# A two-block float32 model on one core: the filter steps regrouped into the projections, and the recurrence of the first block filled with 16 fixed blocks of other matmuls

## The chip, the core and the metric

The kernel is one program on one core of a Trainium2 chip. The metric is the device time of a run in microseconds (us); three runs of the kernel before have a median of 2095.82 us (2094.42 to 2096.31). A run that was profiled gives a trace: for every engine what ran when, and what it waited for. The engines are PE (TensorE matmuls; PEld is its weight load), DVE (VectorE), ACT (ScalarE), POOL (GpSimd) and SP (SyncE), which in this kernel issues nearly all transfers from HBM. Each engine takes its instructions in the order in which the program has them and waits on semaphores.

## The reference, cut to what matters

256 tokens of width 1024, with 16 meta tokens ahead of them, pass two blocks in float32.

```python
# first block
a = rms_norm(h, norm_mix);  p = a @ w_in                       # 1024 x 4096
y_hy = rms_norm(hyena_mixer(p[:, :1536], ...))                 # short conv, 2 long convs through a spectrum of a learned filter
q, f_fwd, f_bwd, i_in, g = split(p[:, 1536:], 5)               # 5 x 512
f = lb + (1 - lb) * sigmoid(f_fwd or f_bwd); k, log_f = 1 - f, log(f)
o = scan(silu(q), k_f, i_in, lf_f) + flip(scan(flipped ..., k_b, lf_b))   # chunks of 64, 4 heads
y_hg = rms_norm_per_head(o) * norm_w * silu(g)
h = h + concat(y_hy, y_hg) @ w_out
h = h + moe(rms_norm(h, norm_ffn))                             # 64 experts, top 2 of the best of 8 groups
h = rms_norm(h, norm_final)[16:]
# second block: five branches, gates, up and out projection
```

Each expert has three matrices of 1024 x 512, 2 MiB each: 384 MiB are read for the experts.

## The kernel before, in words

A framework places instructions on the engines: it takes the program in its order, plays it through and gives each engine a fixed sequence; a helper `_after` adds an order between two instructions that share no data. Nothing of the order is decided on the chip.

**Mixer** (`_phase_a`). Matmuls that need accuracy are done as three fp32r products of high and low halves (`_mm3`); `_split_w` makes the halves of a weight slice, the high one on ACT (L183), the low one on DVE (L184). In the source's order: `hyena_proj(0)`; the filter, for two orders `o`: taps (`fl` from `hids` and `wsh`, `wsl`, times the window `wn`, split again into `sdh`, `sdl`) and five rows of its spectrum (`fl` from `fs`); `hyena_proj(1)`; `to_freq`; `hyena_proj(2)`; `from_freq`; `forget_proj(0)`; then q, v, and after the pools of this stage are closed `forget_proj(1)`, the recurrence `core(d, t)` four times, `g_proj`, and `out_proj(0)`, `out_proj(1)`, the two halves of `w_out`. In `core`, sums of logarithms (`ep`) go to ACT (exp), DVE (products qd, kd, qb, kl), PE (transposes `tp`), then scores `sp`, state updates `up` and outputs `op`. `tok_proj` makes P of 128 x 512 (`mm`), `out_proj` the same (`mo`).

**Weight buffers.** `_load_w` takes the next buffer of a rota, `k.rings`, and issues its 2 MiB on SP. In the mixer the rota is three buffers of the pool `ring`; `early()`, called when the mixer's first pools are closed, puts the two buffers of `ring2` ahead of them. `_moe` then sets the rota anew and asks for the first tiles in this order:

```python
k.rings[at:at] = [p] * n                                  # early: ring2, ring2, ring, ring, ring
k.rings, k.r3 = [r, k.r2, k.r2, r3, r3, r, r], r3         # _body, ahead of _moe
order = [(x, i) for x in range(3) for i in range(4)]      # gate 0-3, up 0-3, down 0-3 of group 0
first.append(load_g(x, 0, i, {3: spare[0], 4: spare[1], 9: spare[2], 10: spare[3]}.get(n)))
if n: _after(k, k.load, prev)                             # issued on SP in this order
```

So the tiles gate 1 and gate 2 take the two buffers of `ring2`; gate 0, up 3 and down 0 take buffers of `ring`; the spares and `ring3` lie where mixer pools lay. A transfer into a buffer waits until the last split of the weight that lay in it.

**Experts.** 16 groups of four experts: gather of tokens (`xp`), gate and up (`gu`), down (`dn`), scatter (`sc`). In the last group dummy matmuls (`warm`, WD = 14 a time) stand between the four steps of down. `finish` adds the four scattered pieces to `h`, multiplies by a gain (`fan`; t = 0 on DVE, t = 1 on POOL), sums squares on ACT, scales (`an`), transposes and starts the second block's first projection. The **second block** follows.

Of the kernel before, what the change touches and what calls it, by code (L numbers as in the profile page):

```python
# [38 lines left out]
def _consts():  # L39
# [27 lines left out]
    win = np.exp((-tt[:, None] * deltas[None, :]).astype(np.float64)).astype(f)[perm]  # L67
# [134 lines left out]
def _phase_a(k, A, early):  # L202
# [194 lines left out]
    for o in range(2):  # L397
        if o:

            later = w3_sums(o)  # L400
            w3_pair()
        sd = [[sp.tile([128, 2, W], F32R, name=f"sd{n}{i}") for n in "hl"] + [sks[i]] for i in range(2)]
        tm = []
        for kt in (2, 0, 1):
            n = 128 if kt < 2 else NM
            for i, (sh, sl, sk) in enumerate(sd):
                ks = slice(kt * 128, kt * 128 + n)
                p = px([128, W], "fl")
                _mm(k, p[:n], hids[:, ks], wsh[:, i], True, False)
                _mm(k, p[:n], hids[:, ks], wsl[:, i], False, True)  # L410
                t = sp.tile([128, W], F32, name="sdt", bufs=2)
                V.tensor_tensor(t[:n], p[:n], wn[:n, kt], op=OP.mult)
                if kt < 2:
                    nc.scalar.copy(sh[:, kt], t)
                    V.tensor_tensor(sl[:, kt], t, sh[:, kt].bitcast(F32), op=OP.subtract)
                else:
                    tm.append(t)
            if kt == 2:

                V.tensor_tensor(tm[0][0:1], tm[0][0:1], tm[1][0:1], op=OP.add)  # L420
                V.tensor_scalar(tm[0][0:1], tm[0][0:1], 0.5, None, op0=OP.mult)
# [4 lines left out]
        for r in range(5):  # L426
# [8 lines left out]
            nc.scalar.copy(H[o][:m, r], p[:m])  # L435

# [106 lines left out]
    hyena_proj(1)  # L543
# [13 lines left out]
    def bound(n):  # L557

        l = VC[n].rearrange("p (r c) -> p r c", r=2)
        e, m = hp.tile([128, 2, 4], F32, name="lbe"), hp.tile([128, 4], F32, name="lbm")  # L560
# [13 lines left out]
        lb = hp.tile([128, 2, W], F32, name="lb")  # L574
        for r, sg in enumerate((0.5, -0.5)):
            nc.scalar.activation(lb[:, r], p, AF.Copy, scale=sg, bias=0.5)
        return lb

    def forget(p, n, lb, ko, fo):
        e = hp.tile([n, W], F32, name="fe")  # L580
        nc.scalar.activation(e, p, AF.Tanh, scale=0.5)
        V.tensor_tensor(e, e, lb[:n, 1], op=OP.mult)
        V.tensor_tensor(fo, lb[:n, 0], e, op=OP.add)
        V.tensor_tensor(ko, lb[:n, 1], e, op=OP.subtract)

    def forget_proj(d):
        lb = bound(("lb_fwd", "lb_bwd")[d])
        P = tok_proj(hcols(1 + d), d == 0)
        for t in range(2):
            forget(P[t], 128, lb, kk[d][:, t], lf[d][:, t])  # L590
        if d == 0:
            meta_sum(mk, P[2])
            forget(mk, NM, lb, mk, ml)
            x = nc.scalar.activation(ml, ml, AF.Ln)
        y = nc.scalar.activation(lf[d], lf[d], AF.Ln)
        if d == 0:
            _after(k, y, x)

    Y = to_freq(uT[0], H[0])
    hyena_proj(2)  # L600
# [23 lines left out]
    P = tok_proj(hcols(0), False)  # L624
    for t in range(2):
        e = _sigmoid(k, hp, P[t], W, tag="fe")
        V.tensor_tensor(q[:, t], P[t], e, op=OP.mult)
# [9 lines left out]
    P = tok_proj(hcols(3), True)  # L637
    for t in range(2):
        nc.scalar.copy(v[:, t], P[t])
    meta_sum(mv, P[2])  # L640
# [19 lines left out]
    def ustate(lhs, rows, src, srows):  # L660
        p = px([128, 4, 128], "up")
        for h in range(4):
            _mm(k, p[:, h], lhs[rows, HS(h)], src[srows, HS(h)], h == 0, h == 3)
# [4 lines left out]
    def core(d, t):  # L668
# [6 lines left out]
        for nm, mi, sc, src in (("qd", 1, 1.0, q), ("kd", 1, -1.0, kk[d]), ("kl", 2, 1.0, kk[d]), ("qb", 0, 1.0, q)):  # L675
            if nm != "kd":
                p = px([128, W], "ep")
                for i, x in enumerate((hi, lo)):
                    _mm(k, p, B3[d][mi], x, i == 0, i == 1)
            ex = hg.tile([128, W], F32, name="ex", bufs=2)  # L680
            nc.scalar.activation(ex, p, AF.Exp, scale=sc)
            r = hg.tile([128, W], F32, name=nm, tag="kl" if nm == "kl" else "kq", bufs=2)
            kq[nm] = r
            if nm == "kl":
                kl = (r, src[:, t], ex)
                continue
# [12 lines left out]
        p = px([128, 4, 128], "sp")
# [10 lines left out]
        for lc in ((0, 1) if d == 0 else (1, 0)):  # L710
# [5 lines left out]
            p = ustate(kq["kl"], rows, v[:, t], rows)  # L716
            S[d][nx] = hg.tile([128, 4, 128], F32, name="S", bufs=SB)
# [51 lines left out]
    def mix_out(P, half, t, cs):  # L769
# [45 lines left out]
    forget_proj(1)  # L815
# [3 lines left out]
    ex = hg.tile([128, W], F32, name="ex", bufs=2)  # L819
    nc.scalar.activation(ex[:NM], p[:NM], AF.Exp)  # L820
    V.tensor_tensor(mk, mk, ex[:NM], op=OP.mult)
    p = ustate(mk, slice(0, NM), mv, slice(0, NM))
    S[0][0] = hg.tile([128, 4, 128], F32, name="S", bufs=SB)
    V.tensor_copy(S[0][0], p)

    core(0, 0)
    core(1, 1)
    core(0, 1)
    core(1, 0)
    g_proj()  # L830
    w += [_load_w(k, wo[h], 4) for h in range(2)]
    out_proj(0, hyT)
# [45 lines left out]
def _moe(k, A, ctx, ps):  # L878
# [233 lines left out]
    def finish(gT, y):  # L1112
# [25 lines left out]
        def scatter(t, n):  # L1138
            p = ps.tile([128, W], F32, name="sc", tag="px")
            m = q(_mm(k, p, gT[:, t], y[n], True, True))  # L1140
            hs = k.h[:, t, n * W:(n + 1) * W]
            q(V.tensor_tensor(hs, p, hs, op=OP.add))
            return m

        def gained(eng, t, n):
            cs = slice(n * W, (n + 1) * W)
            q(eng.tensor_tensor(fan[:, t, cs], k.h[:, t, cs], k.gains[:, 1, cs], op=OP.mult))

        def squares(t, n):
            for j, src in enumerate((k.h, fan)):  # L1150
                sq = mo.tile([128, W], F32, name="nsq")
                q(ACT.activation(sq, src[:, t, n * W:(n + 1) * W], AF.Square, scale=D ** -0.5, accum_out=f(t, 2 * j + n)))
# [35 lines left out]
        gained(V, 0, 0)  # L1188
        scatter(0, 1)
        gained(V, 0, 1)  # L1190
# [4 lines left out]
        gained(G, 1, 0)  # L1195
# [8 lines left out]
        gained(G, 1, 1)  # L1204
# [12 lines left out]
        for t in range(2):  # L1217
            q(G.tensor_tensor(f(t, 4), f(t, 5), k.mhalf, op=OP.pow))
            q(ACT.activation(k.h[:, t], fan[:, t], AF.Copy, scale=f(t, 4)))

    JS = [slice(j * SLOTS, (j + 1) * SLOTS) for j in range(EP)]
    extra = {4: (0, 0), 6: (0, 1), 8: (1, 0), 10: (1, 1)}
    for g in range(k.ngroups):
# [58 lines left out]
        wm = None  # L1282
        for f in range(4):
# [5 lines left out]
            if g == k.ngroups - 1 and f < 3:  # L1289
                wm = warm_up(WD, m, "px")  # L1290
# [3 lines left out]
        if g == k.ngroups - 1:  # L1294
            finish(gT, y)
# [865 lines left out]
```

## Time and profile before

| what | value |
|---|---|
| runs | 2095.82 us median (2094.42 to 2096.31) |
| the profiled execution | 2094.49 us, its span 2092.7 us |
| granted PE clock, mean of the span | 0.945 |
| mixer | 0 to about 252 us |
| experts | to about 1200 us |
| second block | to the end |

The profile's page gives busy times of the engines over the whole span; windows give them for a stretch, with the granted clock of PE (1.00 is 2.4 GHz, 0.50 is 1.2 GHz), the busy share of the 16 DMA engines and what they moved; a timeline lists instructions in order of time, with the idle time ahead of one in brackets and what ended it.

### The profile page before, as it was taken

What the parts mean: (1) busy time and instruction counts of PE and PEld (TensorE: products, weight loads), DVE (VectorE), ACT (ScalarE), POOL (GpSimd) and SP (SyncE); (2) the same over time, 40 slices, a digit from 0 to 9 for tenths busy, and PEclk for the clock granted to TensorE, in tenths of its full rate; (3) what the DMA queues carried; (4) which work ended last, traced back from release to release, by engine and by line L of the source; (5) the groups of instructions that cost most, each with busy time, mean ns of one, the idle gap of its engine ahead of it and who ended that gap; (6) DMA issues with size and microseconds to landing.
All of it is one profiled execution on the core that took longest, in us unless ns stands there. A gap on an engine that the chain in (4) does not pass through costs nothing.

```text
span 2092.7 us, 24267 instructions
## 1 busy us (share of the span) xinstructions
PE 1847.5 (88%) x10132; PEld 1212.4 (58%) x10132; DVE 919.5 (44%) x1521; ACT 652.1 (31%) x976; POOL 69.6 (3%) x89
## 2 busy tenths in 40 slices
PE   8999987678787787876777799999999999999998
PEld 7877832224232331322222379898788788888886
DVE  6886621021111100111111176756666957756756
ACT  5556400002000100000000154546544645446444
POOL 2000000000000000000000020000000100000000
PEclk9999998789899998988988899999999999999999
DMA  8244899999999999999999954455454355454541
GB/s 278 95 159 146 305 398 428 424 404 415 428 423 428 424 427 428 423 427 423 428 426 428 392 182 161 161 180 182 167 185 166 133 190 179 165 180 171 178 159 55
DMA packets 123265, 593.92 MB, mean 284 GB/s; under 512 B 5951, under 2 KB 7264, under 8 KB 101008
## 3 DMA queue, kind: packets, MB, share of 16 engines
q1 hardware_dynamic: 119008, 583.66, 70.3%
q10 hardware_dynamic: 3376, 5.45, 0.8%
q0 software_dynamic: 768, 3.21, 0.4%
q8 instruction: 82, 1.34, 0.3%
q14 instruction: 31, 0.25, 0.0%
HBM read 591.26 MB, written 1.05 MB: 283 GB/s over the span
## 4 chain that ended last, share of the span: by engine, by line
PE 55%; DMA 21%; DVE 3%; issue 1%; ACT 1%; POOL 0%; ACTq 0%; SPq 0%; DVEq 0%; POOLq 0%
PE pt L141 23%; PE gu L141 10%; DMA wring<-in_w_up 8%; DMA wring<-in_w_down 7%; DMA wring<-in_w_gate 6%; PE pT L141 5%; PE pu L141 5%; PE dn L141 5%; PE pw L141 1%; PE ca L141 1%; DVE wp L184 1%; PE ov L141 1%; PE mk L141 1%; PE xp L141 1%; PE warm L141 0%
## 5 line engine op out<-in xcount | busy, mean ns | idle before, releaser
L141 PE MATMUL pt<-wp,ahl 128*128 128x512 f32 x2160 | 516.8, 397 | 1.7 <-DVE wp L184 1.7
L184 DVE TENSOR_TENSOR wp<-wring,wp 128x1024 fp32r<-128x1024 f32 (+1 forms) x368 | 405.7, 1112 | 238.5 <-ACT wp L183 231.2
L183 ACT ACTIVATE wp<-wring 128x1024 fp32r<-128x1024 f32 (+1 forms) x368 | 353.1, 966 | 350.5 <-PE pt L141 176.5
L141 PEld LDWEIGHTS pt<-wp,ahl 128*128 128x128 f32 x2160 | 403.2, 188 | 93.6 <-DVE wp L184 2.5
L141 PE MATMUL gu<-wring,xg 128*32 128x512 f32 x2016 | 322.4, 680 | 122.9 <-DMA wring<-in_w_up 101.3
L141 PEld LDWEIGHTS gu<-wring,xg 128*32 128x32 f32 x2016 | 75.0, 122 | 341.9 <-issue 163.7
L141 PE MATMUL dn<-wring,hT 128*32 128x512 f32 x992 | 186.0, 686 | 65.7 <-DMA wring<-in_w_down 49.9
L141 PEld LDWEIGHTS dn<-wring,hT 128*32 128x32 f32 x992 | 44.2, 118 | 194.2 <-issue 98.3
L1275 DVE SCALAR_TENSOR_TENSOR hh<-th,gu 128x512 f32<-128x512 f32 x16 | 16.9, 1055 | 308.5 <-PE gu L141 308.5
L1293 DVE COPY ye<-dn 128x512 f32<-128x512 f32 x16 | 11.1, 692 | 276.8 <-PE dn L141 276.8
L141 PEld LDWEIGHTS pT<-ahl,wp 128*128 128x128 f32 x960 | 115.6, 189 | 0.5
L141 PE MATMUL pT<-ahl,wp 128*128 128x256 f32 x960 | 115.8, 283 | 0.0
L1280 ACT COPY hT<-hp 128x512 f32<-128x512 f32 x16 | 9.4, 586 | 295.0 <-PE hp L1278 295.0
L141 PE MATMUL pu<-wp,yTh 128*128 128x512 f32 x320 | 98.9, 397 | 0.8 <-ACT yTh L1459 0.6
L1271 ACT ACTIVATE th<-gu 128x512 f32<-128x512 f32 x16 | 9.5, 596 | 250.5 <-PE gu L141 250.5
L1293 ACT COPY ye<-dn 128x512 f32<-128x512 f32 x16 | 9.4, 586 | 242.0 <-PE dn L141 242.0
L141 PEld LDWEIGHTS xp<-oh,hn 128*128 128x128 f32 x512 | 64.0, 200 | 31.1 <-issue 25.7
L141 PE MATMUL xp<-oh,hn 128*128 128x128 f32 x512 | 68.3, 288 | 7.8 <-PEq L1064 4.6
L141 PEld LDWEIGHTS pu<-wp,yTh 128*128 128x128 f32 x320 | 58.7, 188 | 15.6 <-ACT yTh L1459 3.5
L1272 DVE SCALAR_TENSOR_TENSOR th<-th,gu 128x512 f32<-128x512 f32 x16 | 11.0, 687 | 126.1 <-ACT th L1271 126.1
L141 PE MATMUL pu<-wp,yTl 128*128 128x512 f32 x160 | 61.0, 395 | 0.2
L141 PE MATMUL sc<-ye,gT 128*128 128x512 f32 x128 | 59.3, 606 | 0.0
(539 smaller groups left out, 1995.8 us busy)
## 6 DMA issues: line engine op xcount, KB each, us to landing
wring<-in_w_up SPq DMA_DIRECT2D x73, 2048.0 KB, 18.5
wring<-in_w_in SPq DMA_DIRECT2D x63, 2048.0 KB, 7.8
wring<-in_w_gate SPq DMA_DIRECT2D x63, 2048.0 KB, 19.4
wring<-in_w_down SPq DMA_DIRECT2D x62, 2048.0 KB, 20.9
wring<-in_w_out SPq DMA_DIRECT2D x6, 2048.0 KB, 7.9
wring<-in_w_mem_kv SPq DMA_DIRECT2D x4, 2048.0 KB, 17.0
spare<-in_w_down SPq DMA_DIRECT2D x2, 2048.0 KB, 9.6
wring<-in_w_in SPq DMA_DIRECT2D x4, 512.0 KB, 6.2
```

The costliest lines, as they stand in the source:

```text
L141: return k.nc.tensor.matmul(out, a, b, start=start, stop=stop, skip_group_check=True, **kw)
L183: ih = k.nc.scalar.activation(hi, w[:, a:b], AF.Copy)
L184: il = (eng or k.nc.vector).tensor_tensor(lo, w[:, a:b], hi.bitcast(F32), op=OP.subtract)
L1271: nc.scalar.activation(th, P[0], AF.Tanh, scale=0.5)
L1272: V.scalar_tensor_tensor(th, th, 1.0, P[0], op0=OP.add, op1=OP.mult)
L1275: V.scalar_tensor_tensor(hh, by_f(th), 0.5, by_f(P[1]), op0=OP.mult, op1=OP.mult)
L1280: nc.scalar.copy(hT, p)
L1293: (V.tensor_copy if n else nc.scalar.copy)(y[n], P[n])
```

## The change

Seven edits. (1) Each filter's eight steps (three taps, five rows) are called from inside `hyena_proj(1)` and `hyena_proj(2)`, one a weight slice; the window's factor 0.5 is put into the constant, and `wn` is loaded behind the second projection's weight, in two pieces. (2) The projection of q stands at the first `to_freq`, both bounds ahead of it, both `forget_proj` and v behind it. (3) `forget` is written with one scalar_tensor_tensor and two tensor_scalar, and the three logarithms stand together. (4) g's weight is loaded ahead of `early()`. (5) g's projection and `out_proj(0)` become a generator `fillings` of 8 + 8 blocks of six matmuls, of which `core` takes fixed numbers. (6) `w_out` is loaded from within the generator. (7) In `finish` the rows of `h` are put into PSUM ahead of time by matmuls with the identity, and the scatter adds onto them.

```diff
-    nc.sync.dma_start(wn, A["c_win"])
     wz.append(_load_w(k, win_ap[:, :, W:2 * W]))
+    nc.sync.dma_start(wn[:, :2], A["c_win"][:, :2])
+    nc.sync.dma_start(wn[:NM, 2], A["c_win"][:NM, 2])
...
+    hyena_proj(1, filter_steps(0))
+    later = w3_sums(1)
+    w3_pair()
+    hyena_proj(2, filter_steps(1))
...
+    x = forget_proj(1)
+    for a in (ml, lf[0], lf[1]):
+        x = _after(k, nc.scalar.activation(a, a, AF.Ln), x)
+    P = tok_proj(hcols(3), True)
...
+    wg = hcols(4)
+    ws = [_split_w(k, wg, s, s + 1) for s in range(3)]
...
     early()
...
+        p, m = total(1)
+        expo("qd", p, 1.0, q)
+        expo("kd", p, -1.0, kk[d])
+        m = fill(n["qd"], m)
+        if meanwhile:
+            meanwhile(m)
+        turn("qd", m)
+        turn("kd", m)
+        p, m = total(0)
+        expo("qb", p, 1.0, q)
+        p, m = total(2)
+        expo("kl", p, 1.0, kk[d])
+        turn("qb", fill(n["qb"], m))
...
+        m = fill(n["up"], m)
         for h in range(4):
-            _mm(k, O[t][:, h], scm[d][:, h], v[:, t, HS(h)], h == 0 and not begun[t], False)
+            _after(k, _mm(k, O[t][:, h], scm[d][:, h], v[:, t, HS(h)], h == 0 and not begun[t], False), m)
...
+    def fillings():
+        for c in range(8):
+            x = [triples(P[t], (ah[:, c, o:o + 128], al[:, c, o:o + 128]), (wh[:, 0], wl[:, 0]), c) for t, o in enumerate((NM, NM + 128))]
+            yield x[0][0], x[1][2]
...
+        w.extend(_load_w(k, wo[h], 4) for h in range(2))
+        for n in range(2):
+            parts = [_split_w(k, wn, s, s + 1) for s in range(4)]
+            for t in range(2):
+                for cc in (0, 2):
+                    x = [triples(P[t], (hyT[0][:, c, HS(t)], hyT[1][:, c, HS(t)]), (parts[c][0][:, 0], parts[c][1][:, 0]), c)
+                         for c in (cc, cc + 1)]
+                    yield x[0][0], x[1][2]
...
-    g_proj()
-    w += [_load_w(k, wo[h], 4) for h in range(2)]
-    out_proj(0, hyT)
+    core(0, 0, {"qd": 2, "qb": 1, "up": 1}, meta_state)
+    for c in ((1, 1), (0, 1), (1, 0)):
+        core(*c, {"qd": 1, "qb": 1, "up": 1})
+    for _ in filling:
+        pass
...
+            return q(_mm(k, rows[t, n], gT[:, t], y[n], False, True))
...
+            q(V.tensor_tensor(fan[:, t, cs], rows[t, n], k.gains[:, 1, cs], op=OP.mult))
...
+            p = rows[t, n] = ps.tile([128, W], F32, name="sc", tag="px")
+            behind = _after(k, _mm(k, p, k.ident, k.h[:, t, n * W:(n + 1) * W], True, False), behind)
```

SP's queue, before, from behind the two halves of `w_out` (wring_2135, wring_2137), which are issued just ahead of these rows, into `ring`. wring_1581 is the weight of `forget_proj(1)` and wring_2049 that of g, both in `ring2`; the `in_w_gate`, `in_w_up`, `in_w_down` rows are the first tiles of the experts' group 0.

```order
L2117 DMA wr_1542<-in_w_router 128x576 [waits DMASW2_49,DMASW3_49,PE_49,Activation_49]
L173 DMA wring_1581<-in_w_in 128x8x512
L173 DMA wring_2049<-in_w_in 128x8x512 [waits DMAHW6_49]
L173 DMA wring_2460<-in_w_gate 128x4x1024 [waits DMAHW7_49,DMAHW1_49,DVE_49]
L173 DMA wring_2462<-in_w_gate 128x4x1024 [waits DMAHW5_49,DVE_49]
L173 DMA wring_2464<-in_w_gate 128x4x1024 [waits DMAHW6_49,DVE_49,Activation_49]
L173 DMA spare_2456<-in_w_gate 128x4x1024 [waits DMAHW2_49,PE_49]
L173 DMA spare_2457<-in_w_up 128x4x1024 [waits DMAHW3_49,DVE_49,Activation_49]
L173 DMA wring_2468<-in_w_up 128x4x1024 [waits DVE_49,DMAHW4_49,PE_49,Activation_49]
L173 DMA wring_2470<-in_w_up 128x4x1024 [waits DVE_49,PE_49,Pool_49]
L173 DMA wring_2472<-in_w_up 128x4x1024 [waits DVE_49]
L173 DMA wring_2474<-in_w_down 128x4x1024 [waits DMAHW7_49,DVE_49]
```

And of the change, from the first tile on (the g weight, wring_1618, now lies in `ring` and is issued ahead of these rows):

```order
L175 DMA wring_2457<-in_w_gate 128x4x1024 [waits DMAHW0_49,DVE_49]
L2185 DMA wr_1656<-in_w_router 128x576 [waits DMASW2_49,DMASW3_49,PE_49,Activation_49]
L175 DMA wring_1997<-in_w_out 128x4x1024
L175 DMA wring_1999<-in_w_out 128x4x1024
L175 DMA wring_2459<-in_w_gate 128x4x1024 [waits DMAHW7_49,DMAHW1_49,DVE_49]
L175 DMA wring_2461<-in_w_gate 128x4x1024 [waits DMAHW2_49,DMAHW0_49,DVE_49]
L175 DMA spare_2453<-in_w_gate 128x4x1024 [waits DMAHW3_49,PE_49]
L175 DMA spare_2454<-in_w_up 128x4x1024 [waits DMAHW4_49]
L175 DMA wring_2465<-in_w_up 128x4x1024 [waits DMAHW5_49,PE_49]
L175 DMA wring_2467<-in_w_up 128x4x1024 [waits DMAHW6_49,PE_49,Pool_49]
L175 DMA wring_2469<-in_w_up 128x4x1024
L175 DMA wring_2471<-in_w_down 128x4x1024
```

The two halves of `w_out` moved from `ring` into the buffers of `ring2`, and the gate tiles 1 and 2 (wring_2459, wring_2461) wait for their last splits; up 3 and down 0 (wring_2469, wring_2471), which followed `w_out` in `ring`, follow the weights of v and g there.

DVE of the change at the second half of `w_out` (wring_1999), whose last split, into wp_2345, is what wring_2461 waits for; `h` from `mo` are the outputs of `out_proj(1)`, `hT` the router's input:

```order
L186 TENSOR_TENSOR wp_2336<-wring_1999,wp_2336 128x512
L1035 TENSOR_TENSOR before_2513<-c1_60 128x64
L802 TENSOR_TENSOR h_58<-mo0_2268,h_58 128x512
L186 TENSOR_TENSOR wp_2339<-wring_1999,wp_2339 128x512
L802 TENSOR_TENSOR h_58<-mo1_2269,h_58 128x512
L186 TENSOR_TENSOR wp_2342<-wring_1999,wp_2342 128x512
L186 TENSOR_TENSOR wp_2345<-wring_1999,wp_2345 128x512
L787 COPY hT_2320<-tp_2315 128x512
```

In the kernel before the split of the same slice stands at the same place, and down 0 (wring_2474) waits for it.

PE at the filter, before: the taps (`wsh`, `wsl`), then spectrum rows (`sdh`, `sdl`, `sk`) close together, with a few matmuls of `hyena_proj(1)` (`mh`) between:

```order
L141 MATMUL fl<-wsl,hids 128x512
L141 MATMUL mh_642<-ah,wp 128x272
L141 MATMUL mh_642<-al,wp 128x272
L141 MATMUL fl<-sdh_410,fs 128x512
L141 MATMUL fl<-sdl_411,fs 128x512
L141 MATMUL fl<-sdh_410,fs 128x512 x2
L141 MATMUL fl<-sdl_411,fs 128x512
L141 MATMUL fl<-sdh_410,fs 128x512
L141 MATMUL fl<-sdh_412,fs 128x512
L141 MATMUL mh_639<-ah,wp 128x272
L141 MATMUL fl<-sdh_410,fs 128x512 x2
L141 MATMUL mh_640<-ah,wp 128x272
```

And of the change, at the first matmul of a spectrum row:

```order
L143 MATMUL mh_417<-al,wp 128x272
L143 MATMUL mh_418<-ah,wp 128x272
L143 MATMUL mh_418<-al,wp 128x272
L143 MATMUL fl<-sdh_411,fs 128x512
L143 MATMUL fl<-sdl_412,fs 128x512
L143 MATMUL fl<-sdh_411,fs 128x512 x3
L143 MATMUL mh_415<-ah,wp 128x272
L143 MATMUL mh_416<-ah,wp 128x272
```

Between the first tap and the first spectrum row there were 8 matmuls of `mh` before; now there are 32.

## Rows read from the trace of the kernel before

**Rows 1.** Page, part 1: span; busy us of the engines, share, instructions.
```profile
span 2092.7 us, 24267 instructions
PE 1847.5 (88%) x10132; PEld 1212.4 (58%) x10132; DVE 919.5 (44%) x1521; ACT 652.1 (31%) x976; POOL 69.6 (3%) x89
```
**Rows 2.** Windows: length, busy us of PE, PEld, DVE, ACT, POOL; clock, DMA share, GB/s.
```profile
20.00:40.00 20.00, 15.15 (x96) 12.77 (x97) 18.09 (x35) 13.33 (x25) 5.19 (x7) 0.96 1.06 353
40.00:60.00 20.00, 19.44 (x86) 15.07 (x87) 12.21 (x21) 9.46 (x16) 0.00 (x0) 0.87 0.23 64
```
**Rows 3.** Windows, a stretch of the experts.
```profile
600.00:800.00 200.00, 158.39 (x888) 61.79 (x880) 23.89 (x40) 12.82 (x32) 0.00 (x0) 0.93 1.01 426
```
**Rows 4.** Chain that ended last, a piece of the last group: start, us, what.
```profile
1153.82 13.62 DMA wring<-in_w_up
```
**Rows 5.** Timeline of SP's queue: start, us from first issue to last, engine, line, operation.
```profile
151.49 39.81 SPq L173 DMA_DIRECT2D wring<-in_w_gate  x3
205.14 0.37 SPq L173 DMA_DIRECT2D spare<-in_w_gate  x1
211.23 0.37 SPq L173 DMA_DIRECT2D spare<-in_w_up  x1
222.88 6.62 SPq L173 DMA_DIRECT2D wring<-in_w_up  x3
242.86 0.37 SPq L173 DMA_DIRECT2D wring<-in_w_down  x1
250.27 2.80 SPq L173 DMA_DIRECT2D spare<-in_w_down  x2
```
**Rows 6.** Timeline of DVE: the last `yhg`, and the last two splits of `w_out`.
```profile
232.00 0.34 DVE L844 SCALAR_TENSOR_TENSOR yhg<-op,rs,gw 128x128 f32<-128x128 f32 x1
...
241.55 1.28 DVE L184 TENSOR_TENSOR wp<-wring,wp 128x512 fp32r<-128x512 f32 x2
```
**Rows 7.** Windows of 5 us around the mixer's end.
```profile
235.00:240.00 5.00, 5.00 (x21) 3.97 (x22) 3.12 (x5) 1.09 (x2) 0.00 (x0) 1.00 1.03 413
...
245.00:250.00 5.00, 5.00 (x37) 4.57 (x37) 1.66 (x4) 1.31 (x3) 0.55 (x1) 1.00 0.95 377
250.00:255.00 5.00, 4.66 (x42) 4.52 (x41) 2.57 (x12) 3.78 (x4) 0.56 (x1) 1.00 0.72 239
...
260.00:265.00 5.00, 4.56 (x42) 2.78 (x44) 4.24 (x23) 0.67 (x3) 0.00 (x0) 1.00 0.68 223
265.00:270.00 5.00, 5.00 (x41) 2.42 (x42) 1.66 (x5) 0.00 (x0) 0.00 (x0) 1.00 1.01 387
```
**Rows 8.** Timeline of PE: start, us, what; in the filter stage.
```profile
38.56 0.79 PE L141 MATMUL fl<-sdh,fs 128*128 128x512 f32 x1 [4.04 <-ACT sdh L414]
```
**Rows 9.** Timeline of PE, the recurrence: two waits, and the last outputs.
```profile
183.71 0.50 PE L141 MATMUL mm<-wp,ah 128*128 128x512 f32 x1 [1.88 <-ACT wp L183]
...
205.37 0.66 PE L693 MATMUL tp<-ident,qd 128*128 128x128 f32 x4 [0.26 <-DVE qd L687]
...
225.70 1.58 PE L141 MATMUL op<-S,qbT 128*64 128x128 f32 x16
```
**Rows 10.** Timeline of ACT, the recurrence: the logarithm and its table loads.
```profile
177.42 1.28 ACT L595 ACT_TABLE_LOAD   x1
...
180.76 1.28 ACT L681 ACT_TABLE_LOAD   x1
```
**Rows 11.** Timeline of DVE, `finish`.
```profile
1198.36 0.69 DVE L1147 TENSOR_TENSOR fan<-h,gains 128x512 f32<-128x512 f32 x1
...
1200.30 1.28 DVE L1142 TENSOR_TENSOR h<-sc,h 128x512 f32<-128x512 f32 x2
...
1203.34 2.41 DVE L1169 SCALAR_TENSOR_TENSOR an<-fan,fs,gains 128x512 f32<-128x512 f32 x2 [0.65 <-POOL fs L1158]
...
1212.69 1.41 DVE L1169 SCALAR_TENSOR_TENSOR an<-fan,fs,gains 128x512 f32<-128x512 f32 x2 [0.44 <-POOL fs L1158]
```
**Rows 12.** Timeline of POOL, `finish`.
```profile
1203.27 1.27 POOL L1147 TENSOR_TENSOR fan<-h,gains 128x512 f32<-128x512 f32 x1
```

More of the change, by code (lines that the diff above doesn't have):

```diff
@@ L396, in _phase_a, with filter_steps, taps @@
         _after(k, nc.scalar.copy(sk, sk.bitcast(F32)), ends[0])
[L397 to L401, printed above, removed]
+    def filter_steps(o):
         sd = [[sp.tile([128, 2, W], F32R, name=f"sd{n}{i}") for n in "hl"] + [sks[i]] for i in range(2)]
-        tm = []
-        for kt in (2, 0, 1):
+        def taps(kt):
             n = 128 if kt < 2 else NM
+            tm = []
             for i, (sh, sl, sk) in enumerate(sd):
@@ L425, in _phase_a, with row @@
                     V.tensor_tensor(sk[64:80], t[:16], sk[0:16].bitcast(F32), op=OP.subtract)
-        for r in range(5):
+        def row(r):
             m = 128 if r < 4 else 64
@@ L435, in _phase_a @@
             nc.scalar.copy(H[o][:m, r], p[:m])
+        steps = [lambda kt=kt: taps(kt) for kt in (0, 1, 2)] + [lambda r=r: row(r) for r in range(5)]
+        return dict(enumerate(steps))
+    hyena_proj(1, filter_steps(0))
+    later = w3_sums(1)
+    w3_pair()
+    hyena_proj(2, filter_steps(1))
     Fm = const(pa, "fm", [128, 2, 640], later)
@@ L573, in bound @@
         p = p.rearrange("p a b -> p (a b)")
[L574 to L576 removed]
+        lb = hp.tile([128, W], F32, name="lb", bufs=2)
+        nc.scalar.activation(lb, p, AF.Copy, scale=-0.5, bias=0.5)
         return lb
@@ L635, in _phase_a @@
     _rsqrt_mean(k, rh, sst, W, po, tag="rsh")
[L637 to L640, printed above, removed]
     hy1.close()
@@ L658, in _phase_a, with ustate, fill, core @@
     O = [ps.tile([128, 4, 128], F32, name=f"op{t}", tag=f"op{t}", bufs=1) for t in range(2)]
-    def ustate(lhs, rows, src, srows):
+    def ustate(lhs, rows, src, srows, behind=None):
         p = px([128, 4, 128], "up")
         for h in range(4):
-            _mm(k, p[:, h], lhs[rows, HS(h)], src[srows, HS(h)], h == 0, h == 3)
+            k.last_up = _mm(k, p[:, h], lhs[rows, HS(h)], src[srows, HS(h)], h == 0, h == 3)
+            if behind:
+                _after(k, k.last_up, behind)
         return p
     begun = [False] * 2
-    def core(d, t):
+    def fill(n, behind):
+        m = None
+        for _ in range(n):
+            x = next(filling, None)
+            if x:
+                if m is None:
+                    _after(k, x[0], behind)
+                m = x[1]
+        return m or behind
+    def core(d, t, n, meanwhile=None):
         kq = {}
@@ L1108, in overflow, with finish @@
                         V.scalar_tensor_tensor(hs, p, ge[:, t:t + 1], hs, op0=OP.mult, op1=OP.add)
-    def finish(gT, y):
+    def finish(gT, y, rows):
         fan = k.mp.tile([128, 2, D], F32, name="fan", tag="hn")
@@ L1138, in scatter, with gained @@
         def scatter(t, n):
[L1139 to L1145, printed above, removed]
+            return q(_mm(k, rows[t, n], gT[:, t], y[n], False, True))
+        def gained(t, n):
             cs = slice(n * W, (n + 1) * W)
-            q(eng.tensor_tensor(fan[:, t, cs], k.h[:, t, cs], k.gains[:, 1, cs], op=OP.mult))
+            q(V.tensor_tensor(fan[:, t, cs], rows[t, n], k.gains[:, 1, cs], op=OP.mult))
         def squares(t, n):
-            for j, src in enumerate((k.h, fan)):
+            for j, src in enumerate((rows[t, n], fan[:, t, n * W:(n + 1) * W])):
                 sq = mo.tile([128, W], F32, name="nsq")
-                q(ACT.activation(sq, src[:, t, n * W:(n + 1) * W], AF.Square, scale=D ** -0.5, accum_out=f(t, 2 * j + n)))
+                q(ACT.activation(sq, src, AF.Square, scale=D ** -0.5, accum_out=f(t, 2 * j + n)))
         def scale(t):
@@ L1219, in finish, with waiting_rows @@
             q(ACT.activation(k.h[:, t], fan[:, t], AF.Copy, scale=f(t, 4)))
+    def waiting_rows(rows, t, behind):
+        for n in range(2):
+            p = rows[t, n] = ps.tile([128, W], F32, name="sc", tag="px")
+            behind = _after(k, _mm(k, p, k.ident, k.h[:, t, n * W:(n + 1) * W], True, False), behind)
+        return behind
     JS = [slice(j * SLOTS, (j + 1) * SLOTS) for j in range(EP)]
@@ L1294, in _moe @@
         if g == k.ngroups - 1:
-            finish(gT, y)
+            finish(gT, y, rows)
             return
```

122 lines of the change are left out of this document (64 added, 58 removed).

## The prediction

> **What bounds the kernel now.** I read the page's busy times first, then windows by stage, then the waits and queues at the three places that the change touches.
>
> Over the span PE is busy 88% and DVE 44% [rows 1], which would make every gap of PE worth its length. The windows say that this holds by stage only. In the mixer PE is the limit: in 20 to 60 us it stands idle for 4.85 + 0.56 us and loses clock, 0.96 and 0.87 granted of 1.00, which over 20 us each is 0.8 + 2.6 us [rows 2]. In the experts the transfers are the limit: the DMA share is 1.01 at 426 GB/s, while PE is busy 158 of 200 us [rows 3], and in the last group the chain that ended last still runs over the load of an expert's weight [rows 4]. So two rules follow. A gain in the mixer counts only if the experts' transfers start as much earlier, and a tile that goes out late in the stream cannot be made up later, since from there on the queues have no idle time to give.
>
> When does that stream start? SP issues three gate tiles between 151.49 and 191.30, the spare ones for gate 3 and up 0 at 205.14 and 211.23, three more of up from 222.88 to 229.50, and down 0 at 242.86 [rows 5]. Only that last one waits for the end of `w_out`: DVE's last two splits run from 241.55 to 242.83, and the issue follows 0.03 us later [rows 6]. By then eight tiles of 128 x 4 x 1024 floats (2.097 MB) are out. The DMA windows show what this buys: near 413 GB/s in 235 to 240, and idle pieces later, of which more below [rows 7].
>
> **The change, part by part.**
>
> **(a) The order of the first tiles.** In the order listings g's weight leaves `ring2` and `w_out` enters it. Gate 1 and gate 2 take the same two buffers as before, but these now hold the halves of `w_out`, and gate 2 waits for DVE's last split of the second half, the one that released down 0 before. SP takes its queue in order. Behind gate 2 stand gate 3 and up 0 to up 3, whose own buffers are free by then. So of the eight tiles that went out before that split, gate 0 and gate 1 still do, and six do not. The split cannot be much earlier, for it is made in step with the last blocks of `out_proj(1)` on PE.
>
> Price: at the 413 GB/s that the stretch shows [rows 7] a tile takes 2.097 MB / 413 = 5.08 us, six take 30.5. Against it stands what was idle after the split before and will now be filled, the missing part of 413 GB/s in each window: 5 x (1 - 377/413) = 0.4 in 245 to 250, 2.1 in 250 to 255, 2.3 in 260 to 265 and 0.3 in 265 to 270, together 5.1 [rows 7]. Net +25.4. Lower bound: tiles at 426 GB/s [rows 3], 4.92 us each, 29.5, less the same four gaps against that rate, 5.6, is +23.9. Upper bound: no gap is filled, because they come from waits on PE that stay, +30.5. I take 25.4, as six tiles queued at once cover the 22 us in which the gaps lie.
>
> A rule stands beside the row here. By the Trainium skill ("DMA: Bandwidth & Descriptors", Where 436 GB/s comes from) the HBM side at about 358 GB/s per core binds such loads; by that the six would take an estimated 35.1 us and the sum would come out near 2115. The trace disagrees with it, at 426 [rows 3] and 413 GB/s [rows 7].
>
> **(b) The filter among the projections.** PE's first spectrum row waits 4.04 us for ACT's `sdh` [rows 8]; there are now 32 instead of 8 `mh` matmuls between the first tap and it, so this wait should go, and with it the slow clock that follows it. All there is to gain is 4.85 + 0.56 + 0.8 + 2.6 = 8.8 us [rows 2]. Not all of it will come: DVE is busy 18.1 of the 20 us from 20 to 40 and gets no less to do. I take 7, as the one wait and the slow clock are most of the sum; bounds 3 (the wait is cut to half, the clock falls all the same) and 8.8. Moving `wn` behind the second projection's weight on SP's queue, 0.5 MB later, I cost at nothing: taps need it only after a slice of that projection; if this cover fails, it is a part of the lower bound. The projection of q between the spectra and the bounds ahead of it move the same matmuls, nothing.
>
> **(c) The recurrence.** PE waited 1.88 us once for ACT's halves of a weight (`wp`), behind the `ex` that was delayed by a logarithm between exponentials [rows 9], with a table load of 1.28 ahead of the logarithm and one behind it [rows 10]. With the three logarithms together both loads go, and the wait should. The waits at transposes were already filled, 0.26 us at the one after the first outputs [rows 9]. The blocks of g and `out_proj(0)` are the same matmuls at other places: at 21 matmuls in 5.00 us [rows 7] a block of six is 1.4 us. Fixed places may fit worse, so I take 1.5, between 0 (new stalls as large) and 1.9. At the end only 3 of 16 blocks are left after `core`, 4.3 us, while before the last outputs ended at 227.28 [rows 9] and the last `yhg` at 232.34 [rows 6]. That is 5.1 us, part of it queueing on DVE; a loss of up to 0.8 lies within the bounds. One ACT step less per bound, and the rewritten `forget`, are off the path: nothing.
>
> **(d) `finish`.** The additions of `h` (0.69, 1.28 us a pair) leave DVE, and the fan products read PSUM directly; POOL's `fan`, 1.27 us, is gone [rows 11, 12]. DVE does one more pair of products. It waited 0.65 for POOL's `fs` and its first pair of `an` took 2.41 where the pair beside an idle POOL took 1.41 [rows 11], while POOL's `fan` ran from 1203.27 [rows 12]. So 0.7 from the addition ahead of the first fan, 1.0 from the pair, less some of the added products (0.69): 1.2, bounds 0.9 and 1.6. The identity matmuls that put `h` into PSUM stand where PE waits for weights anyway (158 of 200 busy [rows 3]): nothing; without that cover, four matmuls of as many columns as four transposes of 128x128, 0.66 us each by [rows 9], 2.6 us.
>
> **Sum.** The profiled execution took 2094.49 us, 1.3 below the median of the runs. 2094.5 + 25.4 - 7 - 1.5 - 1.2 = 2110.2. Since the measured median may as well lie 1.3 higher, I say **2111**. The range of the forecast alone: 2094.5 + 23.9 - 8.8 - 1.9 - 1.6 = 2106 to 2094.5 + 28 - 3 - 0 - 0.9 = 2119, the 28 being half of the way to the upper bound.
>
> **The rivals.**
> Rival 1, **the mixer gains nothing**: the fixed order stalls PE elsewhere for as much as it saves at 38.56, for example on DVE, which is 90% busy there [rows 2], so that this part of the change does not do what it says. Then 2094.5 + 25.4 - 1.2 = 2119, and 2124 with no gaps filled. Against it: one wait is the largest single item and 24 more matmuls stand ahead of it.
>
> Rival 2, **faster**: the held tiles cost nothing. That is so if the experts' stage does not stand on its stream, or if few tiles are behind the wait. Mixer, recurrence and `finish` gain 9.7 us, or 1.9 tiles at 5.08; with fewer than two tiles behind the split the sign turns. Then 2094.5 - 7 - 1.5 - 1.2 = 2085. For it: the PE share over the span [rows 1]; against it: the DMA share of 1.01 [rows 3] and the order, which has six. [...]
>
> Rival 3, **half of it is made up**: gate 2's buffer comes free some 15 us earlier than I think, because the splits run ahead of PE by half of a projection. Then three tiles' worth less, 25.4 - 15.2, gives 2095, between 2092 and 2103.
>
> **Chances.** Forecast 0.72, rival 1 0.17, rival 2 0.06, rival 3 0.05. About 0.2%, 4 us, is what a measurement of this kernel can tell from no change, so same means 2092 to 2100. Slower takes the forecast, rival 1 and the upper part of rival 3 (0.03), 0.92; same 0.02; faster 0.06. The range of 8 in 10 runs from 2103 (upper end of rival 3) to 2121 (most of rival 1).
>
> **What would show it.** In the changed profile SP's timeline should show gate 0 and gate 1 early, then nothing, then gate 2, gate 3 and four up tiles within a few us behind DVE's last split of `w_out`, near 234 (242.8 less 8.5). DMA share should be low for 20 to 30 us ahead of that and 1.0 after it without the holes of 250 to 265. The windows 20 to 60 should show clock 1.00 and less than 2 us of PE idle; the 1.88 wait should be absent; `finish` should show the first fan product right behind the scatter. The experts' stage should be as long as before, but shifted by +17. Wrong it is if gate 2 goes out before 225, if six tiles take the place of idle time that I took as full, or if the mixer ends later than 250.

## The result and the profile after

The change makes the kernel slower: 2111.58 us, median of 6 runs (2110.21 to 2116.4), against 2096.07 us of the kernel before in the same comparison (2094.42 to 2097.52). The ratio is 1.0078, 95% interval 1.0065 to 1.0091. The prediction said 2111, between 2103 and 2121. All medians leave out one execution, of the run finish_alone below, that took 2187.05 us at a granted clock of 0.819 where its others had 0.942 to 0.948.

The page's first lines of the changed kernel, to be read against [rows 1]:

```profile
span 2109.9 us, 24212 instructions
...
PE 1854.7 (88%) x10108; PEld 1211.4 (57%) x10108; DVE 914.0 (43%) x1517; ACT 649.2 (31%) x972; POOL 68.3 (3%) x87
```

The span is 17.2 us longer, and the shares are the same within a point: the page's first part alone does not tell why. Where the time went is read from three marks that both traces have. The last split of `w_out` on DVE ends the mixer's hold on the buffers; the last `dn` ends the experts; the first group of 48 `pt` is the first after `finish` that runs in one piece. PE's timeline of the kernel before at the last two (start, us, what):

```profile
1194.62 1.92 PE L141 MATMUL dn<-wring,hT 128*32 128x512 f32 x16
...
1220.74 11.31 PE L141 MATMUL pt<-wp,ahl 128*128 128x512 f32 x48
```

and of the change:

```profile
1214.11 1.92 PE L143 MATMUL dn<-wring,hT 128*32 128x512 f32 x16
...
1238.85 11.30 PE L143 MATMUL pt<-wp,ahl 128*128 128x512 f32 x48
```

The last splits on DVE's timeline of the change, against [rows 6]:

```profile
236.04 1.28 DVE L186 TENSOR_TENSOR wp<-wring,wp 128x512 fp32r<-128x512 f32 x2
```

| stretch | before, us | change, us | difference |
|---|---|---|---|
| start to the end of the last split | 242.83 | 237.32 | -5.5 |
| from there to the end of the last `dn` | 953.7 | 978.7 | +25.0 |
| from there to the 48 `pt` (`finish`) | 24.2 | 22.8 | -1.4 |
| from there to the end | 872.0 | 871.1 | -0.9 |

So all that is lost is lost in one stretch. (The 25.0 compares two single executions; the last section says how far such differ.) SP's queue at its beginning, in the change, against [rows 5] (start, us from the first issue to the last):

```profile
146.35 0.37 SPq L175 DMA_DIRECT2D wring<-in_w_gate  x1
166.50 0.34 SPq L2185 DMA_DIRECT2D wr<-in_w_router  x1
166.89 0.98 SPq L175 DMA_DIRECT2D wring<-in_w_out  x2
218.28 19.44 SPq L175 DMA_DIRECT2D wring<-in_w_gate  x2
237.81 0.46 SPq L175 DMA_DIRECT2D spare<-in_w_gate  x1
238.32 0.50 SPq L175 DMA_DIRECT2D spare<-in_w_up  x1
238.92 14.17 SPq L175 DMA_DIRECT2D wring<-in_w_up  x3
253.14 4.91 SPq L175 DMA_DIRECT2D wring<-in_w_down  x1
```

Gate 0 is out at 146, gate 1 at 218. The second of the two in the next line is gate 2: 218.28 + 19.44 = 237.72, that is 0.4 us behind the last split. Gate 3 and up 0 follow within about a microsecond, the other three of up over the next 14 us, one about every 5 us, the time of a transfer. In the kernel before eight tiles were out by 229.5, and only down 0 stood behind the split. The windows of 5 us of the change show the transfers stand still ahead of that point and run without a hole after it (length, busy us of PE, PEld, DVE, ACT, POOL; clock, DMA share, GB/s):

```profile
230.00:235.00 5.00, 5.00 (x23) 4.01 (x22) 3.34 (x7) 1.59 (x3) 0.00 (x0) 1.00 0.01 2
235.00:240.00 5.00, 5.00 (x35) 4.28 (x34) 2.88 (x5) 2.42 (x7) 0.00 (x0) 1.00 0.31 70
240.00:245.00 5.00, 5.00 (x40) 4.66 (x39) 1.94 (x5) 1.53 (x4) 0.55 (x1) 1.00 1.00 404
...
250.00:255.00 5.00, 4.20 (x38) 4.11 (x37) 2.77 (x17) 0.85 (x2) 0.00 (x0) 1.00 1.02 409
...
260.00:265.00 5.00, 5.00 (x42) 2.58 (x38) 1.52 (x4) 0.00 (x0) 0.00 (x0) 1.00 1.02 406
```

Before, 250 to 255 and 260 to 265 had DMA shares of 0.72 and 0.68 [rows 7]; now they have 1.02. So the holes are filled. What is left of the delay is not made up later: in the stretch of [rows 3] the stream runs as before.

```profile
600.00:800.00 200.00, 161.30 (x886) 64.78 (x879) 25.60 (x43) 12.80 (x32) 0.00 (x0) 0.92 1.01 425
```

The mixer did gain. The windows over the filter, against [rows 2], and the stretch behind it:

```profile
20.00:40.00 20.00, 19.10 (x133) 17.42 (x133) 18.87 (x38) 13.84 (x27) 5.17 (x7) 1.00 1.06 354
40.00:60.00 20.00, 20.00 (x125) 17.42 (x124) 14.03 (x24) 12.05 (x21) 0.00 (x0) 1.00 0.52 166
...
80.00:100.00 20.00, 16.72 (x79) 12.78 (x77) 16.89 (x35) 8.46 (x16) 0.00 (x0) 0.91 0.05 20
```

In 20 to 60 PE is idle 0.9 us instead of 5.4, and the granted clock is 1.00 in both windows. But 80 to 100, where PE was busy all the time before, now has 3.3 us of idle PE and a clock of 0.91. PE's timeline there, and DVE's up to the split that it waits for:

```profile
94.73 0.50 PE L143 MATMUL mm<-wp,ah 128*128 128x512 f32 x1 [3.18 <-DVE wp L186]
```

```profile
85.45 0.69 DVE L186 TENSOR_TENSOR wp<-wring,wp 128x512 fp32r<-128x512 f32 x1
86.06 0.68 DVE L522 TENSOR_TENSOR Y<-fz,H 128x512 f32<-128x512 f32 x1
...
93.26 0.67 DVE L528 TENSOR_TENSOR Y<-Y,yt 128x512 f32<-128x512 f32 x1
93.86 0.22 DVE L575 TENSOR_TENSOR lbm<-lbm,lbe 128x4 f32<-128x4 f32 x2
94.00 0.67 DVE L186 TENSOR_TENSOR wp<-wring,wp 128x512 fp32r<-128x512 f32 x1
```

DVE runs without a gap: one split of q's weight, then the thirteen products of the first spectrum, then a step of the bounds, and only then the next split, which ends at 94.67, just before PE goes on. That is a new wait, at the place to which the projection of q was moved.

### The profile page after: what moved, and what is told of

The parts are those of the page before. It is cut to its first block, busy times and chain, and to the rows that moved or that the text cites. A ratio compares the mean times of both kernels' runs of the same rounds, so it can differ in the third digit from the quotient of the medians.

```text
span 2109.9 us, 24212 instructions
## 1 busy us (share of the span) xinstructions
PE 1854.7 (88%) x10108; PEld 1211.4 (57%) x10108; DVE 914.0 (43%) x1517; ACT 649.2 (31%) x972; POOL 68.3 (3%) x87
## 4 chain that ended last, share of the span: by engine, by line
PE 54%; DMA 21%; DVE 2%; issue 1%; ACT 1%; POOL 0%; ACTq 0%; SPq 0%; DVEq 0%; POOLq 0%
PE pt L143 23%; PE gu L143 9%; DMA wring<-in_w_up 8%; DMA wring<-in_w_down 7%; DMA wring<-in_w_gate 6%; PE pT L143 5%; PE pu L143 5%; PE dn L143 5%; PE pw L143 1%; PE ca L143 1%; DVE wp L186 1%; PE ov L143 1%; DMA wring<-in_w_in 1%; PE xp L143 1%; PE mk L143 1%
## 5 line engine op out<-in xcount | busy, mean ns | idle before, releaser
L143 PEld LDWEIGHTS xp<-oh,hn 128*128 128x128 f32 x512 | 63.2, 197 | 30.9 <-issue 25.4
```

The source lines that it names most:

```text
L143: return k.nc.tensor.matmul(out, a, b, start=start, stop=stop, skip_group_check=True, **kw)
```

## The experiments

Each run's ratio is to the kernel before, measured beside it on the same chip; its median there was between 2096.46 and 2096.94 us. The interval behind a ratio is the 95% interval. Between executions the experts' stretch differs by some microseconds (last section), so profiles are compared by stretch.

**rota_mended.** One line of the change: which buffers the first tiles take.

```diff
-            k.rings, k.r3 = [r, k.r2, k.r2, r3, r3, r, r], r3
+            k.rings, k.r3 = [r, r, r, r3, r3, k.r2, k.r2], r3
```

> The change, with the first tiles' buffers dealt out in another order: gate 0 to 2 take the three buffers of ring, up 1 and 2 those of ring3, up 3 and down 0 the two of ring2, where the halves of w_out lay. So only down 0 waits for the last split of w_out, as in the kernel before; nothing else is altered. Theory (six tiles held behind that split, measured 25.0 us between the split and the last group's end): 2111.6 - 25.0 = 2086.6 us, gate 2 out near 195 us, the last dn near 1191. Rival 1 (the experts' stage is longer for another reason, such as the clock or the later weight of w_out): within 3 us of 2111. Rival 2 (half of it): about 2099.

Measured: 2086.24 us (4 runs, 2082.46 to 2092.64), ratio 0.9943 (0.9926 to 0.996). By the medians one line takes back 25.3 us and turns the change from slower to faster than the kernel before; the four runs spread over 10 us, so the size is sure to a few microseconds only. SP's queue shows gate 2 at 186 instead of 237.7, and eight tiles out by 226.3:

```profile
147.31 13.03 SPq L175 DMA_DIRECT2D wring<-in_w_gate  x2
...
186.14 0.37 SPq L175 DMA_DIRECT2D wring<-in_w_gate  x1
201.92 0.37 SPq L175 DMA_DIRECT2D spare<-in_w_gate  x1
207.29 0.37 SPq L175 DMA_DIRECT2D spare<-in_w_up  x1
219.91 6.34 SPq L175 DMA_DIRECT2D wring<-in_w_up  x3
239.64 0.37 SPq L175 DMA_DIRECT2D wring<-in_w_down  x1
```

The profile was taken of the slowest of the four runs, and its last `dn` ends at 1197 where 1191 was expected. The size rests on the runs. Of the 6 us, 2.3 are in the mixer, whose last split ends at 239.60, and a part is a hole in the transfers: in 480 to 490 their DMA share is 0.46, where rota_two_held below has 0.77. What sets the length of the hole was not traced.

**before_rota_held.** The same in reverse, in the kernel before, where the halves of `w_out` lay in `ring`.

```diff
-            k.rings, k.r3 = [r, k.r2, k.r2, r3, r3, r, r], r3
+            k.rings, k.r3 = [r, r, r, r3, r3, k.r2, k.r2], r3
```

> The kernel before, with that one line altered the other way: gate 1 and gate 2 take the buffers of ring in which the halves of w_out lay, up 3 and down 0 those of ring2. Nothing else is altered; six tiles then stand behind DVE's last split of w_out at 242.8. Theory: 2096.1 + 25 = 2121 us, all of it between that split and the last dn. Rival 1: within 3 us of 2096.

Measured: 2121.64 us (4 runs, 2119.29 to 2124.1), ratio 1.0115 (1.0098 to 1.0132), +24.7 us on the median. With none of the change's other edits the kernel before loses the same. Its last split and the issues behind it:

```profile
245.47 1.28 DVE L184 TENSOR_TENSOR wp<-wring,wp 128x512 fp32r<-128x512 f32 x2
```

```profile
150.69 96.46 SPq L173 DMA_DIRECT2D wring<-in_w_gate  x3
247.21 0.50 SPq L173 DMA_DIRECT2D spare<-in_w_gate  x1
247.75 0.50 SPq L173 DMA_DIRECT2D spare<-in_w_up  x1
248.35 8.71 SPq L173 DMA_DIRECT2D wring<-in_w_up  x3
```

```profile
1223.66 1.92 PE L141 MATMUL dn<-wring,hT 128*32 128x512 f32 x16
```

From the split's end, 246.75, to the last `dn`, 1225.58, are 978.8 us: the 978.7 of the change, where the kernel before had 953.7. The same line thus costs in one kernel what it gains in the other, because `w_out` lies in other buffers there. Rival 1 of the expectations, another reason for the longer stage, is out.

**rota_two_held.** The change with two tiles behind the split instead of six.

```diff
-            k.rings, k.r3 = [r, k.r2, k.r2, r3, r3, r, r], r3
+            k.rings, k.r3 = [r, r, r, k.r2, k.r2, r3, r3], r3
```

> The change, with up 1 and up 2 in the two buffers of ring2 (gate 0 to 2 in ring, up 3 and down 0 in ring3), so that of the eight tiles only up 2 and up 3 stand behind the last split of w_out. Theory, a price per held tile: 2086.6 + 2 x 5.08 less 2.5 to 5.1 us of idle time that is filled = 2091.7 to 2094.3. If the wait itself costs, however many tiles are behind it: about 2111. If the stream catches up on a few tiles: 2086.

Measured: 2092.68 us (10 runs, 2091.09 to 2097.24), ratio 0.9984 (0.9975 to 0.9994), 6.4 us above rota_mended. So the price is by the tile, not by the wait, and two tiles are not made up either; the 6.4 has the same few microseconds of doubt, for it rests on rota_mended's median. From the split to the last `dn` the two profiles differ by little (958.4 and 957.5 us), but the windows around the split show the two tiles. Of rota_mended and then of this kernel:

```profile
220.00:240.00 20.00, 19.19 (x113) 15.86 (x113) 14.40 (x32) 8.82 (x24) 2.62 (x3) 1.00 0.86 331
```

```profile
220.00:240.00 20.00, 19.19 (x111) 15.73 (x111) 13.64 (x31) 8.65 (x23) 2.62 (x3) 1.00 0.35 123
```

That is 4.2 MB less, two tiles, while the two windows behind it, to 280, move 400 and 405 GB/s instead of 318 and 376, so that 1.9 MB are still missing at 280: 4.7 us at 413 GB/s. The longer hole of rota_mended's execution at 480 takes back 3.1 us of that.

**rota_mended_pool_splits.** The new wait in the mixer, by taking work off the queue that is late.

```diff
-    P = tok_proj(hcols(0), False)
+    P = tok_proj(hcols(0), False, (2, 3, 4, 5))
...
-            wh, wl = _split_w(k, w, s, s + QS)
+            wh, wl = _split_w(k, w, s, s + QS, G if s in pool else None)
```

> As rota_mended, and in the projection of q four of eight low halves (slices 2 to 5) are split on POOL instead of DVE. In the change PE waits 3.18 us at 94.7 for such a split, which stands behind spectral products on DVE, and loses some 1.7 us of clock behind it. Theory (DVE's queue at that place): the mixer ends 4.9 us earlier, 2081.7. Rival (DVE is full over the whole stretch from 78 to 95, so the wait only moves): less than 2 us of gain, 2085 to 2087.

Measured: 2079.89 us (4 runs, 2078.71 to 2080.71), ratio 0.9917 (0.99 to 0.9933): 6.3 us better than rota_mended by the medians, and the fastest version here. The two intervals overlap a little; the profile settles the mechanism. The mixer's last split ends at 232.37, against 237.32 in the change: 4.95 us earlier, as expected. A window of this kernel:

```profile
80.00:100.00 20.00, 19.61 (x98) 15.49 (x97) 18.16 (x34) 11.43 (x21) 5.93 (x4) 1.00 0.13 39
```

PE's idle time falls from 3.3 to 0.4 us and the clock stays at 1.00, while DVE is as busy as it was (18.2 us, against 17.9 in rota_mended). POOL needs 5.93 us for four splits, 1.48 each where DVE needs 0.68, and PE waits for none of them. So the place of these splits in DVE's queue was the cause.

**bounds_behind_q.** The other way to the same place: both bounds after the projection of q.

```diff
-    lbs = [bound(n) for n in ("lb_fwd", "lb_bwd")]
     P = tok_proj(hcols(0), False)
...
         V.tensor_tensor(q[:, t], P[t], e, op=OP.mult)
+    lbs = [bound(n) for n in ("lb_fwd", "lb_bwd")]
```

> As rota_mended (2086.2), with both bounds behind the projection of q instead of ahead of it. DVE then makes two splits of q's weight ahead of the spectral products instead of one. Theory (PE's wait of 3.18 us comes from the order of DVE's queue, of which the bounds are a part): one more slice, 1.4 us of PE's work, stands ready, so the wait falls below 2 us, and the kernel gains 1.4 to 3 us: 2083 to 2085. Rival (the bounds have no part in it): within 1 us of 2086.2.

Measured: 2082.63 us (6 runs, 2081.09 to 2082.9), ratio 0.9934 (0.9921 to 0.9948). That is just below the theory's range, 3.6 us below rota_mended by the medians. The wait at q fell below 2 us, as the theory said, but another came up in a later projection. PE's timeline:

```profile
94.09 0.50 PE L143 MATMUL mm<-wp,ah 128*128 128x512 f32 x1 [1.58 <-DVE wp L186]
...
140.80 0.50 PE L143 MATMUL mm<-wp,ah 128*128 128x512 f32 x1 [1.39 <-DVE wp L186]
```

So of the 3.2 us at q half is gone, and 1.4 come back. What is gone too is the slow clock behind the first wait:

```profile
80.00:100.00 20.00, 18.42 (x84) 14.15 (x82) 18.26 (x38) 10.93 (x20) 0.00 (x0) 1.00 0.19 62
```

It is 1.00 instead of 0.91. Since the intervals of the two kernels overlap, that is what the profiles show, and the 3.6 us are not certain.

**mended_both.** Both of these edits together.

> rota_mended with both ways of getting q's splits out from behind the spectral products: four low halves on POOL and the bounds behind q. Theory (one cause, one price: the wait and the clock behind it are gone with either): no faster than the better of the two, 2079 to 2082. Rival (two costs on DVE's queue that add up): 2076 to 2077.

Measured: 2081.75 us (6 runs, 2079.3 to 2087.24), ratio 0.9931 (0.9917 to 0.9944). No faster than the better of the two, as the theory said, and the rival's sum is out. But the total hides two things that the profile shows: PE is busy all of 80 to 100, so nothing is left of the wait at q, and the later wait that came with the move of the bounds is there again, 1.40 us at 138.97, where rota_mended_pool_splits has none. The price at q is paid once; the move of the bounds has a small price of its own.

**filter_alone.** The kernel before with the filter's regrouping and nothing else.

```diff
+    hyena_proj(1, filter_steps(0))
+    later = w3_sums(1)
+    w3_pair()
+    hyena_proj(2, filter_steps(1))
```

> The kernel before with the filter's regrouping alone: eight steps called from hyena_proj(1) and hyena_proj(2), the window's factor, wn behind the second weight; q, the bounds, the recurrence and the buffers as before. Theory: the waits and the slow clock in 20 to 60 us go, 7.9 us by the windows of the two profiles, and some 3 to 5 come back at the first spectrum, where hyena_proj(2) no longer fills and a split for the next projection stands behind the products on DVE: 2092 to 2094. Rival 1 (the wait there comes from placing q and the bounds, not from the regrouping): 2088.5 to 2089.5. Rival 2 (nothing gained): 2097.

Measured: 2093.89 us (12 runs, 2089.4 to 2097.24), ratio 0.9988 (0.9978 to 0.9998). The size is the expected one, the place is not. In the profile (of 2089.76 us, one of the fastest) PE is busy all of 80 to 100 and waits for no split at the first spectrum, so that the wait there does come from placing q and the bounds, as rival 1 had it. What comes back comes back later:

```profile
131.57 0.61 PE L143 MATMUL pss<-tri,ysq 128*128 128x1 f32 x4 [2.10 <-ACT ysq L627]
```

with a slow clock around it:

```profile
130.00:140.00 10.00, 8.43 (x34) 6.93 (x35) 7.61 (x21) 7.31 (x13) 1.88 (x3) 0.83 0.52 184
```

In the kernel before PE was busy all of that window, at 1.00. The regrouping moves two projections out of the spectra, and in this execution a wait shows up further on in their place.

**finish_alone.** The kernel before with the edit to `finish` alone.

```diff
+            p = rows[t, n] = ps.tile([128, W], F32, name="sc", tag="px")
+            behind = _after(k, _mm(k, p, k.ident, k.h[:, t, n * W:(n + 1) * W], True, False), behind)
...
+            q(V.tensor_tensor(fan[:, t, cs], rows[t, n], k.gains[:, 1, cs], op=OP.mult))
```

> The kernel before with the edit to finish alone: h put into PSUM by matmuls with the identity, the scatter adding onto it, fan from PSUM on DVE. Theory: 1.4 us between the last dn and the first projection of the second block, as between the two profiles (10.0 against 8.5 us), and nothing elsewhere: 2095.5 against 2096.9, ratio 0.9993. Rival (the 0.9 us that the second block took less in the changed kernel belong to it too): 2094.6.

Measured: 2093.49 us (11 runs, 2090.2 to 2097.76), ratio 0.9987 (0.9976 to 0.9998), which holds both answers. The profiles decide. One wait in the second block, of the kernel before and then of this one:

```profile
1469.66 1.60 PE L141 MATMUL ov<-v,sc 128*128 128x128 f32 x12 [1.57 <-ACT sc L1635]
```

```profile
1469.54 1.60 PE L141 MATMUL ov<-v,sc 128*128 128x128 f32 x12 [0.27 <-ACT sc L1641]
```

All eight profiles of kernels with this edit have the short wait, 0.27 us, and the three without it 1.23 to 1.57. So the 0.9 us that the second block took less belong to this edit, the rival's answer. How it reaches so far was not traced.

**free_blocks.** rota_mended_pool_splits with no block in a fixed place.

```diff
-    core(0, 0, {"qd": 2, "qb": 1, "up": 1}, meta_state)
+    core(0, 0, {"qd": 0, "qb": 0, "up": 0}, meta_state)
...
-        core(*c, {"qd": 1, "qb": 1, "up": 1})
+        core(*c, {"qd": 0, "qb": 0, "up": 0})
```

> As rota_mended_pool_splits (2079.9), with the blocks of g and out_proj(0) in no fixed place: core takes none, and the framework places them where it will among the four cores. Theory of the prediction (the places are worth little, since it had filled the waits before): within 1.5 us of 2079.9. Rival (fixed places fill waits that the framework leaves, above all between up and op): 3 to 6 us slower, 2083 to 2086.

Measured: 2084.35 us (6 runs, 2079.18 to 2087.97), ratio 0.9942 (0.9925 to 0.996). By the median that is the rival's answer, 4.5 us slower; by the trace it is not. The last splits of free_blocks and of rota_mended_pool_splits:

```profile
231.01 1.28 DVE L186 TENSOR_TENSOR wp<-wring,wp 128x512 fp32r<-128x512 f32 x2
```

```profile
231.09 1.28 DVE L186 TENSOR_TENSOR wp<-wring,wp 128x512 fp32r<-128x512 f32 x2
```

The mixers end within 0.1 us of each other. The difference lies in the experts' stretch, 958.0 against 952.6 us, where the two have the same instructions and where other executions differ as much; 2.1 us of it are a hole in the transfers that both have in 470 to 480, with a DMA share of 0.56 here and 0.77 there. That the fixed places are worth nothing in the mixer is shown for these two executions; what they are worth in the runs, whose intervals overlap a little, stays open.

## Why the prediction was right, point by point

**(a) The order of the first tiles** was forecast at +25.4 and measured at +25.0 by the profiles, 25.3 by rota_mended and 24.7 by before_rota_held. Both parts of the term are seen: six tiles wait for the split, and the holes that the sum counted as filled are filled. Of the choice made between the ends, a price per tile at the rate of that very stretch, nothing has to be taken back. The agreement to half a microsecond is luck: the eight profiles in which none of the eight tiles is held have 951.7 to 958.0 us in this stretch, 954.3 in the mean, the two with six held 978.7 and 978.8, so that the six cost about 24.4. The clause that the split "cannot be much earlier" held too.

Two of the signs named for it were missed without harm to the sum. But for gate 1, the transfers stand still for some 60 us ahead of the split and not 20 to 30: the DMA share is 0.00 in 180 to 200 and 0.04 in 200 to 220, and gate 1 itself had to wait till 218. And the last three up tiles are issued over 14 us and not within a few.

The Trainium skill's rule in this part ("DMA: Bandwidth & Descriptors", Where 436 GB/s comes from) had an estimate of 2115. The 404 to 415 GB/s of the change's windows from 240 to 265 disagree with its limit, as those of before did.

**(b) The filter** was forecast at -7 of 8.8. By the same windows it gave 7.9: 4.5 us of idle PE and 3.4 of clock. The step that failed stands at its end, that the projection of q and the bounds ahead of it "move the same matmuls, nothing". The matmuls are the same, but each needs a split from DVE, and DVE is full at the new place. That cost 3.3 us of PE and 1.8 of clock (20 us at 0.91), 5.1 that the sum had at nothing. The run rota_mended_pool_splits shows it from the other side: with four of the splits taken off DVE the mixer ends 4.95 us earlier. `wn` cost nothing, as said, though the weight put ahead of it on SP's queue is 2.1 MB and not 0.5: DVE's first product with it, at 31.78, has no idle time ahead of it.

**(c) The recurrence** was forecast at -1.5. The wait of 1.88 us is gone. The two table loads of [rows 10] are gone from between the exponentials; the ones left stand at 151.99 and 167.67, ahead of the first transposes. But in 150 to 200 the clock is 0.97, 1.5 us less work, against 1.00 before, so of 2.9 us less idle PE there 1.4 remain. Why it falls is open: PE has no idle time in the 50 us ahead of that stretch. The places of the blocks were costed at next to nothing, and the trace of free_blocks shows no other price in the mixer.

**(d) `finish`** was forecast at -1.2 and gave -1.4, and -0.9 more in the second block that no term had. Its two terms are in the trace: the first pair of `an` takes 1.42 us instead of 2.41, and the first fan product starts 1.10 us behind the last `dn` instead of 1.82.

The mixer as a whole came out 3.0 us worse than forecast (-5.5 against -8.5), and even of those 5.5 some 1.2 are luck: the kernel before waited 1.25 us for its first weight at 9.95, the profiled execution of the change did not, that of rota_mended did, for 1.31. `finish` with what follows came out 1.1 better, the tiles 0.4. So the total, 2111.6 against 2110.2 to 2111, is close in part because errors cancel. The sign and the size rest on (a), and that one was shown in both directions, and by the tile.

Rival 1 was half true: the mixer did get a new wait on DVE, but at the first spectrum and not in the stretch of [rows 2], and for 5 us and not for all that the filter gained. Rival 2 is what one line of buffers makes of the change: rota_mended took 2086.24 where the rival said 2085. PE's share over the span, which stood for this rival, was no guide: the 88% hid a stretch that the transfers bound. Rival 3 fell: gate 2 went out 0.4 us behind the split.

## What to carry to other kernels

When weights change places in a ring of buffers, write down for each later load which tenant it waits for, and what stands behind it on the queue that issues in order; with a stage behind that has no idle transfer time, a held load costs its full length, times the number held, less the holes that the late loads fill. A matmul that is moved takes its preparation along: look at the engine that prepares it at the new place, not at the matmuls. And when one term undoes the gains of six others, try that term alone: here one line of seven buffer names was worth 25 us, more than all the rest.

## What the runs showed of the hardware that was not expected

A wait of PE can cost more than its length, and not always the same. The wait of 1.88 us in the recurrence [rows 9] was followed by a full clock in the kernel before:

```profile
180.00:190.00 10.00, 8.12 (x66) 7.14 (x65) 6.25 (x15) 6.45 (x12) 0.00 (x0) 1.00 0.01 2
```

In before_rota_held, with the same wait of 1.88 us at the same matmul, it was followed by this:

```profile
180.00:190.00 10.00, 8.12 (x42) 7.56 (x40) 4.40 (x9) 5.67 (x10) 0.00 (x0) 0.67 0.01 2
190.00:200.00 10.00, 10.00 (x54) 8.22 (x54) 5.25 (x13) 3.86 (x8) 0.00 (x0) 0.82 0.00 1
```

That is 5.1 us of clock for 1.9 of idle time. Two waits of 1.6 and 1.4 us in bounds_behind_q cost none right behind them, the one of 3.18 in the change 1.8 us, and the same one in rota_two_held 3.4 (0.85 in 80 to 100 and 0.98 in the 20 us behind).

The experts' stretch from the last split to the last `dn`, with the same loads in the same order, took from 951.7 us (bounds_behind_q) to 958.0 (free_blocks) in the profiles of kernels that hold no tile of the eight. The length of one hole in the transfers, near 480, is a part of it: the window of 10 us around it has a DMA share of 0.98 in bounds_behind_q and of 0.46 in rota_mended. Differences of 3 to 5 us between single executions of these kernels therefore say nothing by themselves.
